# A two-layer hybrid mixer step: issue order of the first products tied by edges, a first scale chunk of two tiles, the recurrence's transposes one part later, and CV ahead of the last gate columns

## The chip, the core and the metric

The kernel runs on one core of a Trainium2 chip. The metric is the device time of one execution in microseconds; the time before is the median of three runs, 2351.44 us (2345.97 to 2354.68). The profile shows one execution on its own.

A core has five engines that each take their instructions in order from a queue of their own: TensorE (PE: matmuls; PEld is its weight load), VectorE (DVE), ScalarE (ACT), GpSimd (POOL) and SyncE (SP). SP and ScalarE also issue the transfers (DMA). An instruction that waits for a semaphore holds up everything behind it on its engine.

## The reference, cut to what matters

There are 640 tokens: 128 of context and 512 of latents, each kind with its own modulation. Two layers follow each other, each a single mixer:

```
shift, scale, gate = split(silu(cvec) @ w_ada + b_ada)
h = rms_norm(x, norm_g) * (1.0 + scale) + shift
aq, ak, av, ag, bq, bff, bfb, bi, bg, cu, cv, cg = split_proj(h @ w_in)
a_out = attend(q, k, v) * silu(ag)                 # 8 query heads, 2 kv heads, window and sink
b_out = hgrn_mixer(bq, bff, bfb, bi, bg, ...)      # recurrence, 4 heads, two directions
c_out = cu * (w_s @ layer_norm(cv) + b_s) * silu(cg)
y = concat([a_out, b_out, c_out]) @ w_out
x = x + gate * y
```

Widths: D_MODEL is 2048, w_in has 6656 columns, w_ada 6144 (2048 each of shift, scale and gate). All is float32.

## The kernel before, in words

**Tiles.** Tokens stand in NT = 5 tiles of 128, the model's 2048 inputs in KT = 16 tiles of 128 (index k). The normed and modulated input h lies transposed in 16 tiles. A float32 product is made of three cheaper ones: each operand is split into a rounded high part and the rest (hh and hl of h, wh and wl of a weight tile), and the products hh*wh, hh*wl and hl*wh are summed. `wsplit` (L617) makes wh on ScalarE (L621) and wl on VectorE (L622).

**Two forms of projection.** `rowmajor` (L644) multiplies a block of 512 columns: for each k one weight tile of 128 x 512, against the five token tiles (`mm_row`, L633 to L635), into five PSUM banks. `colmajor` (L661) makes 128 columns at a time, transposed, in two banks (`mm_col`, L641, 384 and 256 tokens).

**Side work.** Attention, the recurrence (`hgrn`, L1029) and the gating MLP (`sgu`, L1141) are generators in a list. `tick` runs the next part, up to its yield, of the first of them; a rowmajor block ticks 3 times for most weight tiles, a column tile 8 times, once per 12 of its 24 x 4 matmuls (two k). `flush` runs what is left without projection work between. `fill` runs steps of the filler: the modulation's other columns, computed on VectorE. One step loads a 128 x 512 tile of w_ada and multiplies it into two accumulators (L302). Each weight load of a projection earns `fill_rate` steps.

**What sets the order.** The kernel is written as a sequence of operations on named buffers. At compile time a scheduler orders each engine's instructions by data, free buffers, priority (`hi()` raises it) and its own estimate of when inputs will be there. Each engine then runs this order as it stands. Two calls of the library add edges that fix issue order on one engine and make no instruction wait for another to finish: `keep_in_program_order(x)` puts x behind the last instruction written on x's engine, and `issue_after(x)` puts all that a block writes on x's engine behind x.

**Layer 0's start** (`begin`, L1251). `setup` makes the silu of the conditioning and small constants; `setup2` (L195) and `prep_ctx` (L704) load the rotary tables, masks, sink logits, norm gains and cached keys and values, and convert some of them. Then `first_round` (L401). It loads x transposed in four quarters (L408). `first_norm` (L360) squares the 16 tiles on ScalarE (L366), sums over the inputs with a matrix of ones on TensorE (L368), takes Ln and Exp (L371, L372), and multiplies x by the result on VectorE, one instruction per quarter (L374). The scale half of the modulation is needed in columns, for a chunk of k at a time, `CHUNKS` (L399): 4, 4, 4, 2, 2 tiles. For a chunk, 16 tiles of w_ada (L421) are multiplied with the conditioning (`rows_mm`, L240), copied (L245), turned into columns by small products (L252) and finished on VectorE (`mod_cols`, L287 and L288). `scaled_h` (L376) then makes hh (L383) and hl (L384) of each k. So the round goes: for each chunk, its products with the key and value columns (AK, L633 to L635), with the next chunk's scale rows between them, and then the first columns of CU (L641). The shift is left out of this h and added to the results later. `second_round` (L505) makes the first query columns and computes the shift beside them; L523 and L525 evacuate its banks.

**The rest of a layer** (`layer`, L1291): the other queries, BI, CU and CG columns, then for each of four heads BFF, BFB, BQ and BG; each appends its recurrence to the side list. Then the attention gates AG 0 to 6, a flush, AG 7, CV, the gating MLP as side work under CG 1 and 2 (layer 0) or CU 0 and 1 (layer 1), a flush, and the rest of the C columns. `mul_evac` (L1179) multiplies a result by a gate: the product out of PSUM on VectorE (L1188), exp, `sigma`, and the gate's factor (L1191). `split_mix` (L1200) splits the 16 mixed tiles (L1208, L1209), and `out_proj` (L1213) projects them.

**The recurrence's loop** (L1079). Per head and token tile n: 8 small products build the two directions' attention parts (L1086), VectorE masks them (L1089) and adds them into `asum` (L1091); a yield; TensorE transposes `asum` (L1108) and ScalarE copies it (L1110); a yield; two tiles later the copy is used for the output (L1097, L1100).

Of the kernel before, what the change touches and what calls it, by code (L numbers as in the profile page):

```python
# [8 lines left out]
F32 = mybir.dt.float32  # L9
# [4 lines left out]
ALU = mybir.AluOpType  # L14
# [61 lines left out]
class Net:  # L76
# [160 lines left out]
    def rows_mm(self, acc, lhs, kk, rhs, n):  # L237

        q = kk % 4
        self.nc.tensor.matmul(acc[32 * q:32 * q + 32, 0:n], lhsT=lhs[:, kk, :], rhs=rhs, start=kk < 4, stop=kk >= 12,  # L240
                              skip_group_check=True)
# [118 lines left out]
    def first_norm(self, xm):  # L360
# [11 lines left out]
        nc.scalar.activation(r, r, AF.Exp, scale=-0.5)  # L372
        for m in xm:
            nc.vector.tensor_tensor(m, m, bc(r, 1, 4), op=ALU.mult)  # L374
# [24 lines left out]
    CHUNKS = ((0, 4), (4, 4), (8, 4), (12, 2), (14, 2))  # L399

    def first_round(self, W):  # L401
# [9 lines left out]
        def load_scale(ci):  # L411
# [3 lines left out]
            if ci >= 2:  # L415
                m = self.mg()
                raw += [m[:, i * n:(i + 1) * n] for i in range(2560 // n)]
            while len(raw) < KT:
                raw.append(self.hp.tile([P, n], F32, tag=("hh", "hl")[len(raw) % 2], name=self.nm("wa")))
            for kk in range(KT):  # L420
                nc.sync.dma_start(raw[kk], self.I["w_ada"][0, kk * P:(kk + 1) * P, D + k0 * P:D + k0 * P + n])  # L421
            return raw

        def load_w(ci):
            k0, nk = chunks[ci]
            raw = []
            for k in range(k0, k0 + nk):
                if ci in (0, 2):
# [5 lines left out]
            if ci < 4:  # L434
                if ci in (1, 3):
                    cu = self.wraw([W[k0 * P:(k0 + 4) * P, CU:CU + P]], 4, P)
                else:
                    cu = self.g(512).rearrange("p (a n) -> p a n", n=P)
                    nc.sync.dma_start(cu, W[k0 * P:(k0 + 4) * P, CU:CU + P].rearrange("(a p) n -> p a n", p=P))
                return raw, cu  # L440
            return raw, w[3][1]
# [14 lines left out]
        for ci, (k0, nk) in enumerate(chunks):  # L456
# [5 lines left out]
            raw, cu = w[ci]  # L462
            nn = chunks[ci + 1][1] if ci < last else 0
            ks = range(k0, k0 + nk)
            if ci == last:
# [4 lines left out]
                cw = self.wsplit(cu[:, 2:4], nk, P)  # L470
# [5 lines left out]
                break  # L476
            for k in ks:
                x = self.wsplit(raw[k - k0], 1, 512)
# [4 lines left out]
                for kk in range(m * (k - k0), m * (k - k0 + 1)):  # L483
                    self.rows_mm(acc, self.sc, kk, sc[ci + 1][kk], nn * P)
# [917 lines left out]
```

## Time and profile before

| what | us |
|---|---|
| median of three runs | 2351.44 |
| the profiled execution | 2357.4 |
| its span, first to last instruction | 2355.6 |
| TensorE busy | 2258.8 (96%) |
| TensorE weight load busy | 1969.0 (84%) |
| VectorE busy | 1414.7 (60%) |
| ScalarE busy | 782.5 (33%) |
| GpSimd busy | 290.0 (12%) |
| mean granted TensorE clock | 0.987 |

How to read what follows. A row of the order of time gives start, duration, engine, line, operation, output and inputs, shapes, how often, and in brackets the idle time before it with the instruction that ended it. A float32 matmul has two records. A row of waits gives who waited for whom: the sum, how often, the longest. A row of windows gives the busy time (and count) of PE, PEld, DVE, ACT and POOL in a stretch, then the granted clock, the share of the DMA engines and GB/s. SPq and ACTq are the queues of SP and ScalarE in their role as issuers of transfers.

### The profile page before, as it was taken

The numbers are of one execution on the slowest core, as the hardware profiler recorded it, in microseconds if no ns is written. First come the engines' busy times: TensorE is split into PE (matmuls) and PEld (weight loads), VectorE is DVE, ScalarE is ACT, GpSimd is POOL, SyncE is SP. The second block draws the span as 40 slices with busy tenths as digits, with TensorE's granted clock in tenths as the row PEclk, the third lists the DMA queues.
The fourth block names the chain that finished last, engine by engine and source line by source line (L and its number), as shares of the span: only waits on it lengthen the run. The fifth ranks groups of instructions, "written<-read, shape, count | busy, mean of one in ns | idle before, by whom it ended". The sixth has DMA issues, their size and how long they took to land. (4 is left out here: it accounts for less than half of the span.)

```text
span 2355.6 us, 34870 instructions
## 1 busy us (share of the span) xinstructions
PE 2258.8 (96%) x13276; PEld 1969.0 (84%) x13276; DVE 1414.7 (60%) x2605; ACT 782.5 (33%) x1603; POOL 290.0 (12%) x234
## 2 busy tenths in 40 slices
PE   4999999999999989989999999999999999999999
PEld 2676678899999989877887878799999898998887
DVE  1435887878898877874227445865775942425223
ACT  2223334344343422232224224344343432224111
POOL 0000010100322220111112010100222120101110
PEclk9999999999999999999999999999999999999999
DMA  8556733444444355555332221322332423324332
GB/s 322 182 181 205 253 115 102 141 134 123 135 134 123 113 157 160 169 186 161 108 108 81 80 64 49 104 74 71 109 95 77 121 84 94 99 77 148 103 107 85
DMA packets 262572, 296.41 MB, mean 126 GB/s; under 512 B 17122, under 2 KB 162420, under 8 KB 260612
## 3 DMA queue, kind: packets, MB, share of 16 engines
q1 hardware_dynamic: 252064, 271.27, 37.1%
q10 hardware_dynamic: 10340, 22.91, 3.1%
q8 instruction: 104, 1.70, 0.3%
q14 instruction: 64, 0.52, 0.1%
HBM read 280.38 MB, written 13.73 MB: 125 GB/s over the span
## 5 line engine op out<-in xcount | busy, mean ns | idle before, releaser
L622 DVE TENSOR_TENSOR wl<-wr,wh 128x512 fp32r<-128x512 f32 (+1 forms) x535 | 404.1, 757 | 628.6 <-ACT wh L621 619.7
L621 ACT ACTIVATE wh<-wr 128x512 fp32r<-128x512 f32 (+1 forms) x535 | 336.1, 629 | 953.8 <-PE m L635 542.2
L633 PE MATMUL m<-wh,hh 128*128 128x512 f32 x1440 | 571.6, 397 | 6.9 <-DVE mg L1188 4.2
L634 PE MATMUL m<-wl,hh 128*128 128x512 f32 x1440 | 567.8, 394 | 3.1 <-DVE wl L622 3.1
L635 PE MATMUL m<-wh,hl 128*128 128x512 f32 x1440 | 567.3, 394 | 0.0
L641 PE MATMUL m<-hh,wh 128*128 128x384 f32 x2016 | 478.2, 317 | 1.8 <-ACT g L1350 1.8
L641 PE MATMUL m<-hl,wh 128*128 128x384 f32 x2016 | 463.1, 310 | 0.0
L641 PE MATMUL m<-hh,wl 128*128 128x384 f32 x2016 | 462.6, 310 | 0.0
L302 DVE SCALAR_TENSOR_TENSOR aacc<-wa,s,aacc 128x512 f32<-128x512 f32 x480 | 364.3, 791 | 61.2 <-DMA wa<-in_w_ada_dram 60.0
L633 PEld LDWEIGHTS m<-wh,hh 128*128 128x128 f32 x1440 | 272.6, 189 | 80.4 <-issue 10.3
L635 PEld LDWEIGHTS m<-wh,hl 128*128 128x128 f32 x1440 | 273.2, 190 | 61.3 <-issue 4.9
L634 PEld LDWEIGHTS m<-wl,hh 128*128 128x128 f32 x1440 | 273.5, 190 | 59.5 <-DVE wl L622 4.1
L641 PEld LDWEIGHTS m<-hh,wh 128*128 128x128 f32 x2016 | 312.0, 190 | 9.8 <-issue 6.0
L641 PEld LDWEIGHTS m<-hh,wl 128*128 128x128 f32 x2016 | 309.7, 189 | 1.0 <-issue 0.8
L641 PEld LDWEIGHTS m<-hl,wh 128*128 128x128 f32 x2016 | 310.3, 189 | 0.3
L1071 POOL TENSOR_TENSOR mg<-ev,Dt 128x512 f32<-128x512 f32 x80 | 99.9, 1265 | 461.0 <-DMA wr<-in_w_in_dram 125.1
L1240 POOL TENSOR_TENSOR mg<-mg,ev 128x512 f32<-128x512 f32 x30 | 41.2, 1372 | 288.2 <-DVE ev L1238 284.2
L732 POOL TENSOR_TENSOR mg<-g,g 128x256 f32<-128x256 f32 x32 | 30.7, 978 | 277.3 <-DVE g L730 147.7
L906 ACT ACTIVATE g<-g,st,qs 128x384 f32<-128x384 f32 (+1 forms) x64 | 48.1, 752 | 40.6 <-DVE st L902 40.6
L922 PE MATMUL s<-misc,g 128*128 128x128 f32 x240 | 41.7, 284 | 10.9 <-DVE g L911 10.6
L228 ACT ACTIVATE ev<-ev 128x640 f32<-128x640 f32 x40 | 29.5, 738 | 65.6 <-DVE ev L227 64.4
L926 DVE TENSOR_TENSOR g<-s,g 128x512 fp32r<-128x512 f32 x56 | 38.4, 688 | 20.6 <-ACT g L925 15.0
(272 smaller groups left out, 1954.9 us busy)
## 6 DMA issues: line engine op xcount, KB each, us to landing
wr<-in_w_in_dram SPq DMA_DIRECT2D x406, 256.0 KB, 2.9
wa<-in_w_ada_dram SPq DMA_DIRECT2D x299, 256.0 KB, 2.9
wr<-in_w_out_dram SPq DMA_DIRECT2D x128, 256.0 KB, 2.6
wa<-in_w_ada_dram SPq DMA_DIRECT2D x16, 1024.0 KB, 5.7
wa<-in_w_in_dram SPq DMA_DIRECT2D x9, 1024.0 KB
mg<-const_xT_dram SPq DMA_DIRECT2D x4, 1280.0 KB, 12.8
x<-mg SPq DMA_DIRECT2D x20, 256.0 KB, 2.0
mg<-x ACTq DMA_DIRECT2D x5, 1024.0 KB
```

The costliest lines, as they stand in the source:

```text
L302: nc.vector.scalar_tensor_tensor(acc[:, cd], r, sc, acc[:, cd], op0=ALU.mult, op1=ALU.add)
L621: nc.scalar.activation(wh, raw, AF.Copy)
L622: nc.vector.tensor_tensor(wl, raw, wh.bitcast(F32), op=ALU.subtract)
L633: nc.tensor.matmul(ps, lhsT=hh, rhs=wh[:, 0], start=k == 0, stop=False)
L634: nc.tensor.matmul(ps, lhsT=hh, rhs=wl[:, 0], start=False, stop=False)
L635: nc.tensor.matmul(ps, lhsT=hl, rhs=wh[:, 0], start=False, stop=k == KT - 1)
L641: self.nc.tensor.matmul(ps[hf][:, 0:n], lhsT=w[:, a], rhs=h[:, o:o + n], start=k == 0 and i == 0, stop=k == KT - 1 and i == 2)
L906: nc.scalar.activation(dst[h], src[h], AF.Exp, bias=nmx[:, h:h + 1], scale=rq[:, h:h + 1], accum_out=den[:, h:h + 1])
L922: nc.tensor.transpose(pb[:, h * P:(h + 1) * P], dst[h][:, kb * P:(kb + 1) * P], self.ident)
L926: nc.vector.tensor_tensor(pt[1], pb, pt[0].bitcast(F32), op=ALU.subtract)
L1071: nc.gpsimd.tensor_tensor(k.rearrange("p (i c s) -> p i c s", i=4, c=4), bc(c4(pre[d][0])[:, j], 1, 4), bc(dd, 3, 32), op=ALU.mult)
L1240: (nc.vector if c == 3 else nc.gpsimd).tensor_tensor(xs, xs, y, op=ALU.add)
```

## The change

In `first_round`: the first chunk of four tiles becomes two of two, so there are six. `first_norm` returns its result r and its Exp instead of multiplying x; x is multiplied two tiles at a time (`scale_x`), a chunk ahead of its use, pinned in VectorE's program order for all but the first chunk. The weight splits of all chunks but the last, and the first copy of scale rows, are queued on ScalarE behind the norm's Exp. The scale rows of the next chunk are pinned in TensorE's program order, behind the products of the tile before them. Narrow scale tiles share a buffer.

In `begin`: `setup2` and `prep_ctx` are queued behind the last evacuations of the second round, on ScalarE and on VectorE. The filler's rate goes from 1.25 to 1.0.

In `hgrn`: tile n's `asum` is transposed in the part behind tile n + 1's attention, and its output is made at n + 3 rather than n + 2; a head has one part more.

In `layer`, for layer 0: AG 0 to 5, flush, CV, then AG 6 and 7 as cover for the gating MLP; CG 1 to 3 behind it. Layer 1 keeps its order.

```diff
-        nc.scalar.activation(r, r, AF.Exp, scale=-0.5)
-        for m in xm:
-            nc.vector.tensor_tensor(m, m, bc(r, 1, 4), op=ALU.mult)
+        last = nc.scalar.activation(r, r, AF.Exp, scale=-0.5)
+        return r, last.ins
...
-    CHUNKS = ((0, 4), (4, 4), (8, 4), (12, 2), (14, 2))
+    CHUNKS = ((0, 2), (2, 2), (4, 4), (8, 4), (12, 2), (14, 2))
...
+            i = 0
             while len(raw) < KT:
-                raw.append(self.hp.tile([P, n], F32, tag=("hh", "hl")[len(raw) % 2], name=self.nm("wa")))
+                r = self.hp.tile([P, 512], F32, tag=("hh", "hl")[i % 2], name=self.nm("wa"))
+                raw += [r[:, a:a + n] for a in range(0, 512, n)]
+                i += 1
...
+        def scale_x(ci):
+            k0, nk = chunks[ci]
+            for k in range(k0, k0 + nk, 2):
+                m = xm[k // 4][:, k % 4:k % 4 + 2]
+                x = nc.vector.tensor_tensor(m, m, bc(rrow, 1, 2), op=ALU.mult)
+                if ci > 0:
+                    self.tc.keep_in_program_order(x)
...
-        self.first_norm(xm)
+        rrow, sq = self.first_norm(xm)
         sc[1] = load_scale(1)
+        n0 = chunks[0][1]
         acc = self.bank()
         for kk in range(KT):
-            self.rows_mm(acc, self.sc, kk, sc[0][kk], 512)
-        rows = self.rows_copy(acc, 512)
-        self.mod_cols(0, 1, 0, 4, self.rows_cols(acc, rows, 512))
+            self.rows_mm(acc, self.sc, kk, sc[0][kk], n0 * P)
+        scale_x(0)
+        with self.tc.issue_after(sq):
+            rows = self.rows_copy(acc, n0 * P)
+        self.mod_cols(0, 1, 0, n0, self.rows_cols(acc, rows, n0 * P))
...
             for k in ks:
-                x = self.wsplit(raw[k - k0], 1, 512)
+                with self.tc.issue_after(sq):
+                    x = self.wsplit(raw[k - k0], 1, 512)
...
-                    self.rows_mm(acc, self.sc, kk, sc[ci + 1][kk], nn * P)
+                    self.tc.keep_in_program_order(self.rows_mm(acc, self.sc, kk, sc[ci + 1][kk], nn * P))
+            scale_x(ci + 1)
             rows = self.rows_copy(acc, nn * P)
...
-        for n in range(NT + 2):
+        aTs, sums = {}, {}
+        for n in range(NT + 3):
...
-            if n >= 2:
-                j = n - 2
+            if n >= 3:
+                j = n - 3
...
-            if n < NT:
+            if 1 <= n <= NT:
                 tb = self.bank()
-                nc.tensor.transpose(tb[:, 0:P], asum, self.ident)
+                nc.tensor.transpose(tb[:, 0:P], sums.pop(n - 1), self.ident)
...
-            self.second_round(W)
-        self.setup2()
-        self.prep_ctx(0)
+            act, dve = self.second_round(W)
+        with self.tc.issue_after(act), self.tc.issue_after(dve):
+            self.setup2()
+            self.prep_ctx(0)
...
-        self.fill_rate = 1.25
+        self.fill_rate = 1.0
...
-        for h in range(7):
+        early = 6 if l == 0 else 7
+        for h in range(early):
             self.mul_evac(self.colmajor(W, AG + h * P), self.av_view(h), True)
         self.flush()
-        for h in range(7, 8):
-            self.mul_evac(self.colmajor(W, AG + h * P), self.av_view(h), True)
+        if l > 0:
+            self.mul_evac(self.colmajor(W, AG + 7 * P), self.av_view(7), True)
         self.sgu_evac(self.rowmajor(W, CV))
         self.side.append(self.sgu(l))
         if l == 0:
-            ps = {h: self.colmajor(W, CG + h * P) for h in (1, 2)}
+            ps = [self.colmajor(W, AG + h * P) for h in (6, 7)]
             self.flush()
+            for h in (6, 7):
+                self.mul_evac(ps[h - 6], self.av_view(h), True)
```

More of the change, by code (lines that the diff above doesn't have):

```diff
@@ L239, in rows_mm @@
         q = kk % 4
-        self.nc.tensor.matmul(acc[32 * q:32 * q + 32, 0:n], lhsT=lhs[:, kk, :], rhs=rhs, start=kk < 4, stop=kk >= 12,
-                              skip_group_check=True)
+        return self.nc.tensor.matmul(acc[32 * q:32 * q + 32, 0:n], lhsT=lhs[:, kk, :], rhs=rhs, start=kk < 4, stop=kk >= 12,
+                                     skip_group_check=True)
     def rows_copy(self, acc, n):
@@ L422, in load_scale @@
             return raw
+        cu = {}
         def load_w(ci):
@@ L433, in load_w @@
                     raw.append(r.unsqueeze(1))
-            if ci < 4:
-                if ci in (1, 3):
-                    cu = self.wraw([W[k0 * P:(k0 + 4) * P, CU:CU + P]], 4, P)
-                else:
[L438 to L441, printed above, removed]
+            if k0 % 4 == 0:
+                src = W[k0 * P:(k0 + 4) * P, CU:CU + P]
+                if k0 // 4 % 2:
+                    cu[k0 // 4] = self.wraw([src], 4, P)
+                else:
+                    cu[k0 // 4] = self.g(512).rearrange("p (a n) -> p a n", n=P)
+                    nc.sync.dma_start(cu[k0 // 4], src.rearrange("(a p) n -> p a n", p=P))
+            return raw
+        def scale_x(ci):
[5 more added lines that the diff above has]
+                    self.tc.keep_in_program_order(x)
         sc, w = {}, {}
@@ L461, in first_round @@
                 sc[ci + 2] = load_scale(ci + 2)
-            raw, cu = w[ci]
-            nn = chunks[ci + 1][1] if ci < last else 0
+            raw = w.pop(ci)
+            ca = cu[k0 // 4][:, k0 % 4:k0 % 4 + nk]
             ks = range(k0, k0 + nk)
@@ L469, in first_round @@
                     self.scaled_h(k, xm[k // 4][:, k % 4])
-                cw = self.wsplit(cu[:, 2:4], nk, P)
+                cw = self.wsplit(ca, nk, P)
                 for k in ks:
@@ L522, in second_round @@
             if t % 2:
-                nc.vector.tensor_copy(a, ps[t])
+                dve = nc.vector.tensor_copy(a, ps[t])
             else:
-                nc.scalar.activation(a, ps[t], AF.Copy)
+                act = nc.scalar.activation(a, ps[t], AF.Copy)
+        return act.ins, dve.ins
     def bias_rows(self, W):
@@ L1091, in hgrn @@
                 nc.vector.tensor_tensor(asum, self.att[0], self.att[1], op=ALU.add)
+                sums[n] = asum
                 if n + 1 < NT:
                     K = build(n + 1)
-            if n >= 2:
-                j = n - 2
+            if n >= 3:
+                j = n - 3
                 oo = self.bank()
```

12 lines of the change are left out of this document (5 added, 7 removed).

## The prediction

> **What bounds the kernel now.** I read the page first, then TensorE's waits, then the order of time at the start, then windows around each long wait.
>
> ```profile
> span 2355.6 us, 34870 instructions
> ...
> PE 2258.8 (96%) x13276; PEld 1969.0 (84%) x13276; DVE 1414.7 (60%) x2605; ACT 782.5 (33%) x1603; POOL 290.0 (12%) x234
> ...
> L302 DVE SCALAR_TENSOR_TENSOR aacc<-wa,s,aacc 128x512 f32<-128x512 f32 x480 | 364.3, 791 | 61.2 <-DMA wa<-in_w_ada_dram 60.0
> ...
> mg<-const_xT_dram SPq DMA_DIRECT2D x4, 1280.0 KB, 12.8
> ```
>
> TensorE is busy in 2258.8 of 2355.6 us. The change removes no matmul work, so it can win only the 96.8 us in which TensorE idles, and what its clock loses after an idle stretch. The waits say where that time lies:
>
> ```profile
> PE s L1108 <- DVE asum L1091: 22.4, 12, 5.7
> PE s L368 <- ACT g L366: 17.4, 1, 17.4
> PE s L166 <- DVE g L159: 16.7, 1, 16.7
> PE s L922 <- DVE g L911: 10.6, 8, 3.5
> PE m L633 <- DVE mg L1188: 4.2, 1, 4.2
> ```
>
> Three of the five are in places that the diff touches: the recurrence's transposes (L1108), the norm's sums (L368), and layer 0's first output products, which wait for the last gate's evacuation (L1188). What stands at the start, on TensorE:
>
> ```profile
> 34.77 20.01 PE L368 MATMUL s<-g,ones 128*128 128x384 f32 x64 [17.39 <-ACT g L366]
> 54.71 4.48 PE L240 MATMUL s<-wa,pad 128*32 128x512 f32 x34
> 59.15 1.05 PE L252 MATMUL s<-misc,g 128*128 128x2 f32 x8
> 60.13 3.63 PE L240 MATMUL s<-wa,pad 128*32 128x512 f32 x30
> 64.53 1.05 PE L252 MATMUL s<-misc,g 128*128 128x2 f32 x8 [0.76 <-ACT g L245]
> 67.93 0.79 PE L633 MATMUL m<-wh,hh 128*128 128x512 f32 x1 [2.35 <-ACT hh L383]
> ```
>
> and on ScalarE and VectorE:
>
> ```profile
> 33.47 0.63 ACT L621 ACTIVATE wh<-wr 128x512 fp32r<-128x512 f32 x1 [15.04 <-DMA wr<-in_w_in_dram]
> 34.00 4.48 ACT L366 ACTIVATE g<-mg 128x640 f32<-128x640 f32 x7
> ```
>
> ```profile
> 56.13 11.03 DVE L374 TENSOR_TENSOR mg<-mg,g 128x2560 f32<-128x2560 f32 x4 [15.81 <-ACT g L372]
> 67.08 0.23 DVE L287 SCALAR_TENSOR_TENSOR gs<-s,cols 128x8 f32<-128x8 f32 x2
> ```
>
> Here is the reading that matters most. The norm's squares (L366) do not wait for x. ScalarE takes its instructions in order, and the first weight split (L621) stands ahead of the squares and waits 15.04 us for a weight tile that is loaded last. Once it is free, the squares run seven in a row, so x had been there. Then VectorE multiplies all of x in one block of 11.03 us, and the small scale columns (L287), on which the first product hangs, queue behind it.
>
> **The start.** When could the squares begin?
>
> ```profile
> 1.18 0.42 SPq L408 DMA_DIRECT2D mg<-const_xT_dram x1
> ...
> 7.35 1.30 SPq L408 DMA_DIRECT2D mg<-const_xT_dram x3
> 8.70 18.72 SPq L421 DMA_DIRECT2D wa<-in_w_ada_dram x16
> ```
>
> x's first quarter is issued at 1.18 and the page gives 12.8 us to its landing: 14.0 us. The others, issued by 8.65, land by 21.5 at the same 12.8, and the norm, at 20.01/16 = 1.25 us a tile, asks for the last quarter only 12 tiles or 15 us after its start. With the split queued behind the norm's Exp, the first square ends at 14.0 + 4.48/7 = 14.7, and the sums, at the same 20.0 us, end at 34.7 in place of 54.7. That is the step I trust most; its bounds are 8 us (x as fast as its issue allows, since the moved setup loads no longer share the queue, sums ending near 29) and 21.5 (all of x needed first, sums ending near 42).
>
> From there to the first product. TensorE does 16 scale rows of 256 columns rather than 512:
>
> ```profile
> 105.39 1.06 PE L240 MATMUL s<-wa,pad 128*32 128x512 f32 x8
> ...
> 114.41 0.64 PE L240 MATMUL s<-mg,pad 128*32 128x256 f32 x8
> ```
>
> By 0.64/1.06 these take 0.60 of the 3.63 us, 2.2 us. Then the copy with its hand-over, 64.53 - 63.76 = 0.77; four small column products, half of 1.05, 0.5; and from the scale columns to the first product 67.93 - 67.08 = 0.85. Sum 4.3 us. VectorE's side is shorter: from the sums' end to the multiply's start 56.13 - 54.72 = 1.4, and two of sixteen tiles cost 11.03/8 = 1.4. The two weight splits that now come after the Exp fit between on ScalarE (0.63 us each). So the first product comes at 39.0, not at 67.93: 28.9 us earlier.
>
> Not all of this is won. Before its first product the old kernel had also done the second chunk's rows and columns, 3.63 + 1.05, and half of the first chunk's, 2.2 + 0.5: 7.4 us of matmuls that hid under the 11 us multiply and now stand between products. Two more chunk boundaries appear, each with the copy, columns and scale to pass under two column tiles; the bounds are 0 and the 2.35 of the old first wait, and I take 0.5 each, since the old boundaries inside the round show no wait. Net 28.9 - 7.4 - 1.0 = 20.5 us.
>
> The multiplies that leave the block are 1.4 us each in VectorE's slack between products. SP's queue gains 16 more, smaller issues; 16 whole ones took 18.72 us while waiting for the setup's small loads, and half the bytes have until 34.7. Here a rule of the Trainium skill speaks against the change: DMA: Bandwidth & Descriptors, section Bandwidth, says to batch transfers to 1 MiB or more, and its fit gives 2.3 us for 128 KB; one after another, 16 such would land near 46 us and put the first product at 50, 11 us of the gain lost. The row above disagrees with the "one after another": 16 transfers of 256 KB were issued in 18.72 us, so they overlapped, at 1.2 us each.
>
> The clock is a second point:
>
> ```profile
> 60.00:80.00 20.00, 16.89 (x81) 11.71 (x82) 13.53 (x19) 7.07 (x15) 0.00 (x0) 0.83 0.74 243
> 820.00:840.00 20.00, 14.35 (x115) 13.06 (x114) 17.73 (x28) 4.79 (x10) 6.97 (x6) 0.91 0.50 148
> 1020.00:1040.00 20.00, 12.74 (x43) 9.31 (x43) 15.97 (x24) 5.79 (x10) 1.68 (x1) 0.83 0.70 248
> 1880.00:1900.00 20.00, 15.46 (x124) 13.92 (x125) 11.41 (x26) 4.83 (x12) 9.69 (x9) 0.83 0.23 63
> ```
>
> After idling 0.76 + 2.35 us the granted clock means 0.83 over 20 us, a loss of 3.4 us. The new gap is 4.3 - 2.2 - 0.5 = 1.6 us, shorter; but nothing here says that it is short enough, and I let the 3.4 us stand. The Trainium skill (TensorE: Matmul & The Clock Gate, What's actually happening) has the clock fall only after an idle window of about 3.4 us; by that the start would win 3.4 us more.
>
> **The recurrence.** The sum of the two attention parts is transposed one part later.
>
> ```profile
> 835.82 0.45 PE L1108 MATMUL s<-misc,asum 128*128 128x128 f32 x1 [5.65 <-DVE asum L1091]
> ```
>
> ```profile
> 1884.54 0.45 PE L1108 MATMUL s<-misc,asum 128*128 128x128 f32 x1 [5.47 <-DVE asum L1091]
> ```
>
> ```profile
> 1894.37 1.76 PE m L641 x12
> ```
>
> Between two parts of a head lie 12 projection matmuls, 1.76 us. The transpose now follows its sum by three such stretches rather than one, so it has 3.5 us more (two by 1.76). Of the 12 waits the two longest keep 5.65 - 3.5 and 5.47 - 3.5, together 4.1; the ten others sum to 22.4 - 11.1 = 11.3, mean 1.1, and go. That is 18.3 us, and with the clock (0.91 and 0.83 over 20 us lose 1.8 and 3.4) up to 23.5. But VectorE is late at these places (17.73 of 20 us busy, and the filler's multiplies wait 60.0 us in all for their loads, in VectorE's queue). Some of the lateness will come up at the next thing that TensorE wants from it; I take two thirds of 23.5, 15 us. Bounds: 0 and 23.5. A head needs one part more, 35 rather than 34, four heads 140; the columns ahead of the flush offer 144 in layer 0 (18 tiles by 8), so nothing spills out.
>
> **The end of layer 0.** CV moves ahead of AG 6 and 7, and these cover the gating MLP in place of CG 1 and 2; so all three CG tiles lie between it and the output projection, rather than one.
>
> ```profile
> 1022.12 3.75 DVE L1209 TENSOR_TENSOR hl<-mg,hh 128x640 fp32r<-128x640 f32 x5
> 1025.80 0.87 DVE L1188 TENSOR_TENSOR mg<-mg,m 128x384 f32<-128x384 f32 x2
> ```
>
> VectorE reached the last evacuation (L1188) only after five splits, while TensorE needed its bank. The window from 1020 has 7.3 us idle and 3.4 us of clock lost, 10.7. With two more tiles of cover the earlier gates are out of the way, but the splits still end in the same order. I take half, 5 us; bounds 0 and 10.7.
>
> **The filler's rate, 1.25 to 1.0 steps a weight load.** A step is two multiplies of 0.791 us, so VectorE has a fifth less of it while layer 0 projects, and more in the output projection. A fifth of the 10.6 us of attention waits is 2 us; bounds 0 and 5.
>
> **The setup behind the second round.** Nine loads on ScalarE's queue, and VectorE's conversions that wait for them, now come after the evacuation of the first query half. Queued behind them are ScalarE's weight splits, and TensorE waits for these.
>
> ```profile
> ACT mg L525 <- DMA g<-in_cache_k_dram: 2.1, 1, 2.1
> ```
>
> Four of the nine stood there already, and one held ScalarE for 2.1 us, with no wait on TensorE. I charge 2 us; bounds 0 and 10 (five more by 2.1).
>
> **Sum.** -20.5 - 15 - 5 - 2 + 2 = -40.5 us. The profiled execution took 2357.4 us, so 2316.9 for such a one; it stood 0.25% above the median of the runs, and the same ratio, 0.983, on 2351.44 gives 2311.
>
> **Rivals.** *The recurrence gains nothing* (0.13): VectorE's lateness is work, not order, and TensorE waits as long at the next evacuation. For it: VectorE's 17.73 of 20 us. Against: at 1880 it is busy 11.41 of 20 only. -40.5 + 15: 2326.
>
> *The start gains nothing* (0.08): the scale rows arrive late, because their smaller loads wait for one another, and the first product stays where it was. For it: 18.72 us went into issuing 16 loads. Against: a weight tile issued behind x and a whole scale chunk had landed by 33.47, before the sums' new end at 34.7. -40.5 + 20.5: 2331. The rule on batching above would make half of this loss.
>
> *All waits in reach go* (0.06): 28.9 - 7.4, 23.5, 10.7, 5: about -61, 2291.
>
> *The edges do not give the order that they name, or the rest of the program is ordered anew and new waits eat the gain* (0.09): 2347.
>
> *Slower* (0.05): pinned scale rows stall the products.
>
> ```profile
> SPq L421 <- PE s L240: 15.3, 5, 7.6
> ```
>
> Each chunk's rows are now tied behind the products before them, and the next products stand behind the rows on TensorE. If a chunk's loads come late, because the loads wait for buffers (five times, up to 7.6 us), TensorE waits too. At all five boundaries, with the clock's 3.4 us: 5 x 11 = 55 us, -40.5 + 55 = +14.5: 2366. It decides from 40.5/5 - 3.4 = 4.7 us a boundary (7.1 for half a percent). Against it: these waits of SP left TensorE without a wait.
>
> **Chances.** Forecast 0.59, rivals as given. Half a percent, 11.8 us, is about what a measurement of this kernel can tell from no change. Faster: 0.59 + 0.13 + 0.08 + 0.06 = 0.86; same 0.09; slower 0.05. The forecast's own range, from the bounds of the unknown costs, is 2296 to 2326. The range given reaches the two smaller gains and the largest, 2288 to 2338.
>
> **What would show it.** Right: the squares start near 14 us, the sums end near 35, the first product (the old L633) starts near 39; the sum of waits for asum is under 6 us; the wait for the last gate's evacuation is shorter. Wrong: the squares still begin behind a weight split; a wait of the scale rows for loads; waits for attention or weight splits that grew by what asum's lost.

## The result, and the profile after

The changed kernel takes 2338.84 us (median of 7 runs, 2336.47 to 2342.52), the kernel before 2353.25 in the same comparison; the ratio is 0.9945, 95% interval 0.9931 to 0.9960. That is 13 us or 0.55% faster, just beyond what a measurement can tell from no change, where 40 us were forecast; the time lies 0.8 us outside the range. One run of the kernel before at 2788 us, and one at 5726 us in the comparison of runs 13 to 16, are left out of the ratios; without the first, its median is 2352.3 us. The profiled execution took 2338.18 us.

First the page of the kernel after: its span, the busy times, the filler's multiplies and the loads of x.

```profile
span 2336.4 us, 34944 instructions
...
PE 2261.4 (97%) x13308; PEld 1968.0 (84%) x13308; DVE 1424.3 (61%) x2612; ACT 778.7 (33%) x1605; POOL 293.9 (13%) x234
...
L302 DVE SCALAR_TENSOR_TENSOR aacc<-wa,s,aacc 128x512 f32<-128x512 f32 x480 | 368.6, 801 | 72.9 <-DMA wa<-in_w_ada_dram 72.3
...
mg<-const_xT_dram SPq DMA_DIRECT2D x4, 1280.0 KB, 5.8
```

TensorE is as busy as before (2261.4 against 2258.8 us), so the 19.2 us between the two spans are idle time. The filler's multiplies wait longer for their loads, 72.3 us instead of 60.0. That goes with the lower rate: of the runs below with two buffers and all loads, those at 1.25 have 60.5 (run 1) and 53.7 (run 4), those at 1.0 between 70.7 and 78.5. Why is open. The start, on TensorE and then on ScalarE:

```profile
11.96 19.26 PE L368 MATMUL s<-g,ones 128*128 128x384 f32 x64 [1.72 <-DVE g L184]
31.15 1.93 PE L240 MATMUL s<-wa,pad 128*32 128x256 f32 x32
33.90 0.61 PE L252 MATMUL s<-misc,g 128*128 128x2 f32 x4 [0.81 <-ACT g L245]
35.94 0.73 PE L652 MATMUL m<-wh,hh 128*128 128x512 f32 x1 [1.44 <-ACT hh L382]
```

```profile
11.06 0.21 ACT L181 ACTIVATE g<-g 128x16 f32<-128x16 f32 x1 [1.89 <-DVE g L180]
11.19 4.47 ACT L366 ACTIVATE g<-mg 128x640 f32<-128x640 f32 x7
```

The squares start at 11.19 us (34.00 before), right behind the setup's last activation (L181), which waits for VectorE; the sums end at 31.2 (54.7), the first product (L633 before, L652 now) starts at 35.94 (67.93): 32.0 us earlier. Because some matmuls that used to hide now stand between products, the fair measure is a count: the 400th projection matmul (L633 to L635 and L641 before, L652 to L654 and L660 after) ends 24.5 us earlier than before. The same count taken further down both traces tells where the lead goes: 26.5 us at the 2000th, 37.9 at the 3400th, in the last head of layer 0's recurrence, 28.3 at the 3552nd, the last before the two kernels go on with different columns, 21.0 at the 4272nd, where layer 0's columns end, 16.1 at the 5200th, near the end of layer 0's output projection, and 19.2 at the end. So the recurrence did win another 11 us, and lost 9.6 of them at its last step. Part of such a lead can be side work that is only put off. TensorE's idle time up to the same products leaves that out: it is shorter than before by 23.2, 24.4, 33.0, 26.7, 22.2, 21.3 and 21.8 us at these seven places. What it was lost to, TensorE's waits say (engine, line waited for, us in total, times, longest):

```profile
PE s L1143 <- DVE g L1137: 10.4, 6, 6.1
PE s L166 <- DVE g L159: 9.5, 1, 9.5
PE s L941 <- DVE g L930: 8.7, 6, 3.2
PE s L1072 <- ACT g L1068: 7.7, 2, 4.1
PE m L652 <- DVE mg L1208: 5.3, 1, 5.3
PE s L1193 <- DVE mg L1194: 5.1, 1, 5.1
...
PE s L1128 <- DVE att L1108: 1.9, 1, 1.9
```

The wait for `asum`, 22.4 us before, is gone altogether. In its place stand three that before had 0.3, 0 and 0: a head's last transposes wait for the scaling of their input (L1143 for L1137), the products on kT for its copy (L1072 for L1068), and the moved transposes for the attention copy (L1128 for L1108). These are 10.4 + 7.7 + 1.9 = 20.0 us. The wait at the last gate's evacuation is 5.3 rather than 4.2, and the gating MLP's output (L1193) waits 5.1 rather than 1.0. What VectorE did ahead of the longest of them:

```profile
835.18 2.74 DVE L302 SCALAR_TENSOR_TENSOR aacc<-wa,s,aacc 128x512 f32<-128x512 f32 x4 [2.05 <-DMA wa<-in_w_ada_dram]
837.84 0.28 DVE L1124 COPY g<-s 128x128 f32<-128x128 f32 x1
...
840.86 4.01 DVE L302 SCALAR_TENSOR_TENSOR aacc<-wa,s,aacc 128x512 f32<-128x512 f32 x4 [0.94 <-DMA wa<-in_w_ada_dram]
844.79 0.68 DVE L641 TENSOR_TENSOR wl<-wr,wh 128x512 fp32r<-128x512 f32 x1
845.40 0.28 DVE L1124 COPY g<-s 128x128 f32<-128x128 f32 x1
845.60 0.73 DVE L302 SCALAR_TENSOR_TENSOR aacc<-wa,s,aacc 128x512 f32<-128x512 f32 x1
846.26 1.06 DVE L1137 TENSOR_SCALAR g<-g,oss 128x128 f32<-128x128 f32 x5
```

```profile
846.59 0.47 PE L1143 MATMUL s<-misc,g 128*128 128x128 f32 x1 [6.08 <-DVE g L1137]
```

VectorE takes its queue in order. Ahead of the last output copy (L1124) and the scaling (L1137) stand eight filler multiplies in two groups, 6.75 us of work, with 2.05 and 0.94 us of waiting for their loads. The Trainium skill says the same of the queue (Perfetto Trace Analysis, the section Per-engine timelines: VectorE, ScalarE and GpSimd are strictly first in, first out), and this trace agrees: TensorE had finished the last product to be copied at 834.75 us (L1120), and its copy starts at 845.40. The other wait, for the kT copy, runs over ScalarE:

```profile
1839.73 0.75 ACT L1206 ACTIVATE ev<-m 128x384 f32<-128x384 f32 x2
1845.53 0.74 ACT L228 ACTIVATE ev<-ev 128x640 f32<-128x640 f32 x1 [5.05 <-DVE ev L227]
1846.30 0.74 ACT L229 ACTIVATE ev<-ev 128x640 f32<-128x640 f32 x1
1846.94 0.61 ACT L640 ACTIVATE wh<-wr 128x512 fp32r<-128x512 f32 x1
1847.46 0.58 ACT L1068 ACTIVATE g<-s 128x512 f32<-128x512 f32 x1
```

A column tile ends at 1839.7. Its evacuation needs VectorE (L227), which is late; ScalarE stands 5.05 us behind that, and the kT copy stands behind ScalarE's evacuation, though TensorE's transposes for it (L1067) had run from 1841.93 for 0.60 us. The stretches with these waits also lose clock (the windows' rows; the third number from the end is the mean granted clock, the last two are the DMA share and GB/s):

```profile
840.00:860.00 20.00, 13.92 (x74) 13.07 (x73) 16.33 (x29) 4.97 (x12) 1.96 (x1) 0.83 0.48 144
930.00:950.00 20.00, 14.82 (x89) 14.63 (x90) 16.86 (x30) 2.78 (x6) 0.03 (x1) 0.83 0.51 157
1000.00:1020.00 20.00, 13.67 (x52) 10.47 (x51) 15.67 (x23) 9.30 (x17) 3.76 (x3) 0.83 0.65 221
```

0.83 over 20 us is at most 3.4 us lost in each. Some of it falls into the idle time itself: in the first window the clock is at half from 845.0 to 851.6 us, and TensorE idles until 846.6.

### The profile page after: what moved, and what is told of

Same layout as the page of the kernel before. It is cut to its first block, busy times and chain, and to the rows that moved or that the text cites. A ratio compares the mean times of both kernels' runs of the same rounds, so it can differ in the third digit from the quotient of the medians.

```text
span 2336.4 us, 34944 instructions
## 1 busy us (share of the span) xinstructions
PE 2261.4 (97%) x13308; PEld 1968.0 (84%) x13308; DVE 1424.3 (61%) x2612; ACT 778.7 (33%) x1605; POOL 293.9 (13%) x234
## 4 chain that ended last, share of the span: by engine, by line
PE 75%; DVE 12%; DMA 7%; issue 2%; ACT 1%; POOL 0%; DVEq 0%; ACTq 0%; POOLq 0%
PE m L660 29%; PE m L652 11%; PE m L653 11%; PE m L654 11%; DMA wa<-in_w_ada_dram 6%; DVE aacc L302 4%; DVE wl L641 2%; PE s L240 2%; PE s L895 1%; PE s L941 1%; PE s L1105 1%; PE s L1072 1%; PE s L953 1%; PE s L954 1%; PE s L319 1%
## 5 line engine op out<-in xcount | busy, mean ns | idle before, releaser
L641 DVE TENSOR_TENSOR wl<-wr,wh 128x512 fp32r<-128x512 f32 (+1 forms) x535 | 401.5, 752 | 575.2 <-ACT wh L640 566.7
L652 PE MATMUL m<-wh,hh 128*128 128x512 f32 x1440 | 571.6, 397 | 9.2 <-DVE mg L1208 5.3
L654 PE MATMUL m<-wh,hl 128*128 128x512 f32 x1440 | 565.6, 393 | 0.0
L660 PE MATMUL m<-hh,wh 128*128 128x384 f32 x2016 | 478.1, 317 | 0.0
L660 PE MATMUL m<-hl,wh 128*128 128x384 f32 x2016 | 465.0, 311 | 0.0
L660 PE MATMUL m<-hh,wl 128*128 128x384 f32 x2016 | 464.6, 311 | 0.0
L302 DVE SCALAR_TENSOR_TENSOR aacc<-wa,s,aacc 128x512 f32<-128x512 f32 x480 | 368.6, 801 | 72.9 <-DMA wa<-in_w_ada_dram 72.3
L652 PEld LDWEIGHTS m<-wh,hh 128*128 128x128 f32 x1440 | 272.0, 189 | 84.5 <-issue 10.3
L654 PEld LDWEIGHTS m<-wh,hl 128*128 128x128 f32 x1440 | 272.4, 189 | 59.0 <-issue 2.6
L660 PEld LDWEIGHTS m<-hh,wh 128*128 128x128 f32 x2016 | 312.5, 190 | 9.8 <-issue 8.1
L660 PEld LDWEIGHTS m<-hl,wh 128*128 128x128 f32 x2016 | 311.5, 189 | 0.4
L660 PEld LDWEIGHTS m<-hh,wl 128*128 128x128 f32 x2016 | 311.1, 189 | 0.3
L1090 POOL TENSOR_TENSOR mg<-ev,Dt 128x512 f32<-128x512 f32 x80 | 95.7, 1213 | 321.5 <-PE s L1105 107.2
L228 ACT ACTIVATE ev<-ev 128x640 f32<-128x640 f32 x40 | 29.5, 738 | 72.3 <-DVE ev L227 71.2
L945 DVE TENSOR_TENSOR g<-s,g 128x512 fp32r<-128x512 f32 x56 | 38.4, 687 | 24.0 <-ACT g L944 18.1
L1045 POOL TENSOR_TENSOR g<-g,EG 128x512 f32<-128x512 f32 x16 | 22.7, 1416 | 239.4 <-DVE Dt L1030 125.1
```

What stands on the lines that cost most here:

```text
L302: nc.vector.scalar_tensor_tensor(acc[:, cd], r, sc, acc[:, cd], op0=ALU.mult, op1=ALU.add)
L641: nc.vector.tensor_tensor(wl, raw, wh.bitcast(F32), op=ALU.subtract)
L652: nc.tensor.matmul(ps, lhsT=hh, rhs=wh[:, 0], start=k == 0, stop=False)
L654: nc.tensor.matmul(ps, lhsT=hl, rhs=wh[:, 0], start=False, stop=k == KT - 1)
L660: self.nc.tensor.matmul(ps[hf][:, 0:n], lhsT=w[:, a], rhs=h[:, o:o + n], start=k == 0 and i == 0, stop=k == KT - 1 and i == 2)
L945: nc.vector.tensor_tensor(pt[1], pb, pt[0].bitcast(F32), op=ALU.subtract)
```

## The experiments

Each run is set against the kernel before on the same chip; ratios have their 95% interval. Line numbers differ by one or two between the kernels. "Parts" are the pieces into which a head's work is cut, laid between column matmuls.

**1. The new start alone**: the changed kernel with the loop, the column order and the rate of before; the setup edge stays.

```diff
-        for n in range(NT + 3):
+        for n in range(NT + 2):
...
-        self.fill_rate = 1.0
+        self.fill_rate = 1.25
...
-        early = 6 if l == 0 else 7
-        for h in range(early):
+        for h in range(7):
```

> The kernel before with the first round's edges and two-tile chunks and with the setup behind the second round; recurrence, columns' order and filler rate as before. Theory A (VectorE's lateness only moves): the start is worth what the profiles show at the 400th projection matmul, 24 us, and the rest of the change nothing or less, so this is 24 us below the kernel before, about 2329, faster than the changed kernel. Theory B (the recurrence is worth the 15 us that were forecast, and another part of the change takes them back): the same 2329 here, since neither is in it. Theory C (a rebuilt order is worth plus or minus 10 us whatever is edited): anywhere from 2320 to 2345.

Measured: 2332.7 us, 0.9912 (0.9894 to 0.9930). The start by itself is faster than the whole change. The other edits together cost about 6 us.

**2, 3, 4. One edit undone each**, in the changed kernel: the old loop (2), the old column order (3), the old rate (4).

```diff
-                nc.tensor.transpose(tb[:, 0:P], sums.pop(n - 1), self.ident)
+                nc.tensor.transpose(tb[:, 0:P], asum, self.ident)
```

> The changed kernel with the old recurrence loop. Theory A: the waits go back from the last transposes (L1143 of the changed kernel) to those of asum, and the time stays, 2339 plus or minus 4. Theory B: 15 us slower than the changed kernel, 2354.

Measured: 2331.8 us, 0.9906 (0.9888 to 0.9924). The new loop costs 7 us. The waits of the kernel with the old loop:

```profile
PE s L1127 <- DVE asum L1110: 9.9, 6, 5.3
...
PE s L1142 <- DVE g L1136: 4.1, 2, 3.9
```

With 1.4 us of waiting for GpSimd (L1105 for L1090) these are 15.4 us in the recurrence, where the new loop has 20.0. Neither expectation had a gain.

```diff
-            ps = [self.colmajor(W, AG + h * P) for h in (6, 7)]
+            ps = {h: self.colmajor(W, CG + h * P) for h in (1, 2)}
```

> The changed kernel with AG 7 before CV and CG 1 and 2 under the gating MLP, as before. Theory A: the wait for the last evacuation ahead of the output projection is about as long either way (4.2 before, 5.3 after), so 2339 plus or minus 4. Theory B, the forecast's own term: 5 us slower, 2344.

Measured: 2331.2 us, 0.9908 (0.9888 to 0.9927). The new order costs 7.7 us, which neither expectation had; without it the wait at the gating MLP is gone from the list, and the one at the last evacuation is 4.6 us.

> The changed kernel with the filler at 1.25 steps again. The profiles lose about 8 us between the 1400th and the 2000th row product, in layer 0's output projection, where the filler now runs on. Theory A: with 1.25 it ends sooner there and some of the 8 us come back, but VectorE is later in the recurrences: 2330 to 2340. Theory B with the filler as the part that takes the gain back: 2329. The forecast's own term for the rate: 2 us slower, 2341.

Measured: 2338.6 us, 0.9936 (0.9921 to 0.9952): no difference. With the new loop and order, the rate is worth nothing.

**5, 6. Filler without its loads**: fifteen of sixteen loads of the filler's weight tiles are left out, in the changed kernel (5) and with the old loop (6). Every multiply is still done, on a tile that is there already, so the gates and layer 1's modulation are not the reference's.

```diff
-            with self.hi():
-                r = self.arp.tile([P, 512], F32, tag="ar", name=self.nm("wa"))
+            if k == 0:
+                with self.hi():
+                    r = self.arp.tile([P, 512], F32, tag="ar", name=self.nm("wa"))
```

> The changed kernel, but each of the filler's blocks loads one tile and multiplies it sixteen times: 15 of 16 of the filler's loads are left out, so its outputs (gates, and layer 1's modulation) are not the reference's; all multiplies stay. Theory A, in the form that the filler's load waits in VectorE's queue (72 us in all after the change) put VectorE late: TensorE's waits for L1137, L1194, L1208 and L1068 (28 us after the change) fall below 10, and the time to 2315 or less. Theory A2, that the filler's multiplies alone (369 us) are what stands ahead: the waits stay above 18, 2332 or more.

> The same as the kernel with one load a block (15 of 16 filler loads left out), with the old recurrence loop. If VectorE is no longer late (theory A), the position of the transposes is worth under 4 us either way against that kernel. Theory B, the forecast's: the old loop waits for asum again, 10 to 15 us slower than that kernel.

Measured: 2304.9 us (5; 0.9789, 0.9771 to 0.9807) and 2292.6 (6; 0.9736, 0.9716 to 0.9757). The loads are worth 34 us of the whole. Not all of this need be their waits: 63 of 296 MB of traffic are gone with them (the pages of the two kernels). The new loop costs 12 us without them too, which neither expectation had, so they are not what makes it slow. Its rows in 5, and then those of 6:

```profile
PE s L1144 <- DVE g L1138: 6.0, 5, 2.2
PE s L1129 <- DVE att L1109: 5.4, 3, 3.3
PE s L1073 <- ACT g L1069: 5.0, 2, 2.5
```

```profile
PE s L1128 <- DVE asum L1111: 7.3, 8, 1.7
...
PE s L1106 <- POOL mg L1091: 2.2, 4, 0.8
```

16.4 against 9.5 us, and none of the old loop's waits for `asum` is longer than 1.7. The gating MLP's wait fell to 1.3 in 5 and that of the last evacuation to 3.1: those two do come from the loads. The four waits that run 5 was to bring from 28 us to below 10 (for the scaling, the kT copy, the gating MLP and the last evacuation) still make 15.4.

**7. Start, setup edge and rate**, with the old loop and the old order (the first run with the rate at 1.0).

```diff
-        self.fill_rate = 1.25
+        self.fill_rate = 1.0
```

> The kernel before with the start's edges, the setup behind the second round and the filler at 1.0; recurrence and columns' order as before. If the parts are separate: undoing the recurrence alone won 7 us and undoing the columns' order alone 7.7, so both undone is 2339 - 14.7 = 2324. If the two shared one cause (each undone removes the same loss): 2332, as the start alone gave. Theory C, order by luck: outside 2320 to 2336.

Measured: 2321.6 us, 0.9859 (0.9841 to 0.9877). Here the rate is worth 11 us, five times what the forecast gave it. The `asum` rows of run 1, and then of run 7, show where:

```profile
PE s L1127 <- DVE asum L1110: 22.1, 12, 5.7
```

```profile
PE s L1127 <- DVE asum L1110: 9.7, 6, 5.3
...
PE s L1142 <- DVE g L1136: 4.2, 2, 3.9
```

Rate and loop were aimed at the same wait, and the rate takes 12.4 of its 22.1 us; 4.2 come up at the scaling.

**8, 9, 11. A third buffer for the filler's loads**, on run 7; room for it comes from single buffers for `So` and `asum` and a scratch tile done away with.

```diff
-        self.arp = ec(tc.tile_pool(name="arp", bufs=2))
+        self.arp = ec(tc.tile_pool(name="arp", bufs=3))
```

> The kernel with the start's edges and the filler at 1.0, recurrence and order as before, and three buffers rather than two for the filler's loads; to make room, asum and the state copy have one buffer and the squares of the recurrence's output are written into its output tile. Theory A (load waits make VectorE late): the filler's load waits fall from over 60 to under 25 us and the time by 5 to 10 us below the same kernel with two buffers. If the loads are late for another reason (their place in SP's queue, behind other waits): no change, plus or minus 4.

Measured: 2328.2 us, 0.9886 (0.9865 to 0.9907), slower. The filler began inside the start:

```profile
50.09 0.79 PE L652 MATMUL m<-wh,hh 128*128 128x512 f32 x1 [15.01 <-ACT hh L382]
```

So in 9 the filler's first multiply is tied behind the second round, and 11 adds the new column order.

```diff
-                    nc.vector.tensor_scalar(acc[:, cd], r, sc, None, op0=ALU.mult)
+                    with self.tc.issue_after(self.behind) if (l, blk) == (0, 8) else nullcontext():
+                        nc.vector.tensor_scalar(acc[:, cd], r, sc, None, op0=ALU.mult)
```

> The kernel with three filler buffers, with one more edge: the filler's first multiply is queued on VectorE behind the second round. Without that edge the third buffer put filler work into the start (TensorE waited 20 us for L382 there), but from the 400th projection matmul on that kernel was 16 us faster than the one with two buffers. Theory A (load waits make VectorE late): the start is whole again and the 16 us stay, 2306 plus or minus 4. If the 16 us came from the filler having begun early: 2318 to 2322.

> The kernel with three filler buffers and the tied filler, with the new columns' order (CV ahead of AG 6 and 7). If the order's cost of 8 to 10 us came from the filler's load waits beside the gating MLP: within 3 us of the same kernel with the old order. If it lies in the order itself: 8 to 10 us slower than that.

Measured: 2312.7 us (9; 0.9823, 0.9806 to 0.9841) and 2312.1 (11; 0.9820, 0.9803 to 0.9838). The load waits in VectorE's queue, in the waits of run 9:

```profile
DVE aacc L303 <- DMA wa<-in_w_ada_dram: 18.1, 14, 4.8
```

18.1 us rather than 75.2 in run 7, and the new order now costs nothing and brings nothing, where with the same loop and two buffers it costs 10 us (run 2 against run 7): its loss in the change came from late loads. These are the fastest of the kernels that compute the whole reference, 26 us below the changed one.

**10. One part more at the tail**: run 3 (new loop, old order) with an empty part ahead of a head's last transposes, 36 parts a head.

```diff
             nc.vector.tensor_scalar(oj, oj, ss[:, j:j + 1], None, op0=ALU.mult)
         yield
         yield
+        yield
```

> The changed kernel with the old columns' order (2331.2) and the new recurrence loop, with one empty part more ahead of a head's last transposes, so that VectorE's scaling (L1137) has 1.76 us more. If the new loop's cost of 7 to 12 us lies at that place alone: 5 us or more faster, 2326 or less. Theory A (lateness only moves to whatever asks next): the waits for L1137 shrink, others grow, 2331 plus or minus 4.

Measured: 2314.8 us, 0.9841 (0.9819 to 0.9863), 16 us faster than run 3. The recurrence's waits of run 3, then of run 10:

```profile
PE s L1143 <- DVE g L1137: 11.7, 6, 7.7
...
PE s L1072 <- ACT g L1068: 7.1, 2, 3.9
...
PE s L1128 <- DVE att L1108: 1.9, 1, 1.9
```

```profile
PE s L1128 <- DVE att L1108: 3.8, 2, 1.9
PE s L1144 <- DVE g L1137: 3.6, 3, 2.8
```

20.7 us became 7.4. The scaling's wait was to go and mostly went; that the kT copy's went too was not expected.

**12. The setup edge taken off** run 7.

```diff
-        with self.tc.issue_after(act), self.tc.issue_after(dve):
-            self.setup2()
-            self.prep_ctx(0)
+        self.setup2()
+        self.prep_ctx(0)
```

> The kernel with the start's edges and the filler at 1.0 (2321.6), with the setup and the cached keys free to be issued early again. Their place behind the second round costs 2.7 us of wait for the cached keys and 1.7 us of clock; at the start, their small loads held SP's queue for 10 us before. If the edge only costs: 2317. If it is what lets x come early: the first sums end some us later and the time is 2322 to 2328.

Measured: 2321.7 us, 0.9864 (0.9847 to 0.9882). The edge is worth nothing; the traces show two effects that about cancel. Without it VectorE waits until 10.20 us for the load of the attention sinks (L220), ahead of the silu of the conditioning, and the first product comes at 37.82 us rather than 35.45 in run 7. With it, TensorE waits 2.7 us for the cached keys (L738) in run 7, and in run 12 it does not.

**13 and 14. The part more elsewhere**: in run 7, with the old loop (13, 35 parts), and in the changed kernel whole (14, 36 parts); the edit is that of run 10.

> The kernel with the new start, the setup edge and rate 1.0, the old recurrence loop and the old column order (2321.6 us without this edit), with one empty part more before a head's last transposes. If the extra part alone made the gain of 16 us of the kernel with the new loop and that part, this one comes out near 2314 (2311 to 2317), and the later asum transposes are worth nothing. If the later transposes pay only once the tail has a part more, this one stays at 2321.6 (within 4), because the old loop waits 9.7 us for the asum tile and only 4.2 for the scaling, and the part takes away those 4.2 at most.

> The changed kernel whole (new column order too) with one empty part more before a head's last transposes. If the tail was what the new loop lost by, in any order: 2338.8 less the 16 us that the same edit gave with the old order, 2323 (2318 to 2328). If the new order's load waits take the gain back (the wait of 5.1 us at the gating MLP and 5.3 at the last evacuation stay): nearer 2330.

Measured: 2322.9 us (13; 0.9855, 0.9831 to 0.9879) and 2325.3 (14; 0.9862, 0.9842 to 0.9882). With the old loop the part brings nothing; in the changed kernel it brings 13.5 us by the medians. And in 13 a wait appears that the old loop with 34 parts does not have:

```profile
PE s L1072 <- ACT g L1068: 7.1, 2, 4.7
```

Every run with 35 parts a head, the old loop or the new, has this wait (4.9 to 7.7 us), none with 34 or 36 does. A column tile holds eight parts; the number of parts sets where the fourth head's kT products fall against a tile's end.

**15 and 16. Third buffer and part more**: run 9 with the part at the tail (16), and with the new loop as well (15; two `asum` buffers, made room for by narrower constant tiles).

> Third filler buffer tied behind the second round (2312.7 us with the old loop), with the new loop and the extra part at the tail, old column order. The new loop's two edits together gave 7 us against the old loop where loads were late; with loads in time the asum waits that they take away are 6.7 us in 8. If that holds with three buffers: 2306 (2302 to 2310). If TensorE in layer 0 is bound by VectorE's total work up to the gating MLP, so that waits only move: 2312 (within 3).

> Third filler buffer tied behind the second round, old loop, with the extra part at the tail alone. The profile without that part shows one wait of 5.2 us for the scaling and 6.7 us for the asum tile. If the part takes away the first: 2307 (2304 to 2310); if the wait moves to the asum tile or to the last evacuation: 2312 (within 3).

Measured: 2321.3 us (15; 0.9842, 0.9824 to 0.9861) and 2319.3 (16; 0.9844, 0.9822 to 0.9866), against 0.9823 for run 9: both miss, and the two gains do not add up. Run 16 has 35 parts and the kT wait (5.9 us). In run 15 the moved transposes wait 7.4 us for the attention copy.

**17 and 18. The same number of parts, placed otherwise**: the empty part at a head's start rather than its tail, in run 3 (17), and two of them in run 7, with the old loop (18). Both have 36.

```diff
         pre = []
+        yield
```

> The kernel with the new loop and the old column order (2331.2 us), with the empty part more at the start of each head rather than at its tail: 36 parts a head, the tail as it was. If the gain of 16 us came from the room ahead of the last transposes, it is not here: 2331 (2327 to 2334). If it came from where the parts fall against the column tiles of eight parts (with 35 parts the fourth head's products on kT fall one part behind a tile's end, with 34 and 36 they don't), it is here too: 2315 (2312 to 2319), and TensorE's wait for the kT copy, 7.1 us in 2, is gone.

> The kernel with the new start, the setup edge, rate 1.0, the old loop and the old column order (2321.6 us with 34 parts a head, 2322.9 with 35), with two empty parts at the start of each head: 36. If the later transposes are worth nothing once the number of parts is alike, this one equals the kernel with the new loop and 36 parts, 2315 (2312 to 2318). If the number of parts matters only with the later transposes, it stays at 2322 (2319 to 2325). No wait for the kT copy in either case.

Measured: 2327.6 us (17; 0.9883, 0.9864 to 0.9903) and 2330.5 (18; 0.9895, 0.9879 to 0.9912). The rows of 17, then those of 18:

```profile
PE s L1129 <- DVE att L1109: 8.4, 3, 3.1
...
PE s L1144 <- DVE g L1138: 4.5, 1, 4.5
PE m L660 <- DVE ev L988: 3.9, 2, 2.7
```

```profile
PE s L1129 <- DVE asum L1112: 19.4, 18, 2.3
...
PE s L1144 <- DVE g L1138: 3.0, 1, 3.0
```

In 17 the kT wait is gone as the theory of parts had it, but only 3.6 us of the time, within the uncertainty: most of run 10's gain hung on the place at the tail. In 18 the old loop is 9 us slower with 36 parts than with 34; neither expectation had that. The wait for `asum` doubled, 9.7 to 19.4 us, though the part that follows the sum is the same: only the place against the column tiles moved. The six kernels that differ only in loop and parts, from their traces; the waits are all the idle time ahead of the recurrence's own products and transposes (us):

| loop, parts a head | waits in the recurrence | TensorE idle in all | time |
|---|---|---|---|
| new, 36, at the tail (10) | 7.7 | 52.5 | 2314.8 |
| old, 34 (7) | 15.2 | 59.8 | 2321.6 |
| old, 35, at the tail (13) | 17.3 | 61.4 | 2322.9 |
| new, 36, at the start (17) | 14.5 | 65.6 | 2327.6 |
| old, 36, at the start (18) | 22.4 | 70.8 | 2330.5 |
| new, 35 (3) | 21.1 | 65.6 | 2331.2 |

The time follows TensorE's idle time, roughly, and neither the loop nor the number of parts alone. The waits in the recurrence are not all of it: in 17, column tiles wait 3.9 us for an evacuation (L660 for L988) besides. With 36 parts in both and the empty ones at the start, the new loop has 8 us less waiting than the old (17 against 18), and 2.9 us less time, which the two intervals do not tell from none.

## Why the prediction was right in direction and wrong in size

**The start** was forecast at -20.5 us. Run 1 gives -22 (2332.7 against 2354 to 2355), the trace's count 24.5. Its mechanism held: the squares stand no longer behind the split, and the sums end at 31.2 (34.7 forecast) and the first product starts at 35.9 (39.0). One reading in it was wrong. x does not set the squares' start: its first quarter lands 6.1 us after its issue rather than 12.8, at 7.3 us, and the squares begin at 11.19 behind the setup's work, 2.8 us before the forecast's 14.0; that is the 3. The pauses ahead of the first product are 2.25 us where 1.6 were forecast. The sixteen smaller loads overlapped, as the row of before had said: sixteen were issued in 14.60 us, each took 3.3 us to land (median of the page), and no scale row waited for them. The rival *slower*, pinned rows that stall, did not come.

**The step that failed is the recurrence's**: "Some of the lateness will come up at the next thing that TensorE wants from it; I take two thirds of 23.5, 15 us. Bounds: 0 and 23.5." The first half was right and better than forecast: `asum`'s wait fell from 22.4 to nothing (with the rate at 1.25 too, run 4). But 20.0 us came up elsewhere, at the scaling and the kT copy above all, and the lower bound of 0 left out a loss. Beside the old loop in the same kernel, the edit cost 7 us (run 2), 10 with the old order (run 3 against 7) and 12 without loads (5 against 6).

What the runs show in place of the step is that the waiting moves to whatever TensorE wants next, and that its sum depends on where a head's parts fall. The step counted the part more as free, since 140 parts fit in 144 slots. It moved the heads' steps against the tiles' ends: at 35 parts the kT copy queues behind an evacuation that waits for VectorE (7.7 us here; 7.1 with the old loop in 13, where other waits shrank and the time stayed). One part more at the tail brings 16 and 13.5 us back with the new loop (10 and 14) and nothing with the old (13); two empty parts cost the old loop 9 us (18); and against that one the new loop, also with 36 parts and its empty one at the start, loses nothing (17). So the 7 to 12 us are the price of the later transposes together with their part, and not of later transposes as such.

That the old wait had been cover, in which VectorE and ScalarE caught up ahead of the head's tail, fits the gain of the part at the tail, but no run shows it by itself. The rival *the recurrence gains nothing* had the mechanism, lateness as work. Its argument against, VectorE only 11.41 of 20 us busy, failed because the 20 us reach far behind the wait: in the kernel before, during the wait of 5.47 us that ends at 1884.54, VectorE was busy from 1879.43 to 1884.39, and in the rest of the window it stood 6.4 us waiting for TensorE's products (L1086).

**The end of layer 0** was forecast at -5 with bounds 0 and -10.7; it cost 7.7 (run 3), or 10 with the old loop (run 2 against 7). The wait at the last evacuation went from 4.2 to 5.3 and a second one, 5.1, came at the gating MLP. Run 11 shows that the order is neutral once the loads are in time.

**The rate** was sized at -2 from attention's waits (L922 before), which it left nearly alone (10.5 in run 1, 9.1 in run 7). It acts on `asum`: -11 with the old loop and order (run 7), 0 with the new ones (run 4). The sum added two edits that act on the same wait.

**The setup edge** was charged 2 and is worth 0 (run 12): the charge was about right (2.7), but the 2 us that the edge wins at the start were left out.

By the runs, step by step: -22 (run 1), -11 (run 7), +10 (the new loop, run 3), +8 (the new order, the changed kernel): -15 or so, and 13 to 14 are measured. Such steps run from one kernel to the next and must add up; in another order the shares differ. With the rate at 1.25, for one, the new loop and order together cost 6 us (run 4 against run 1) rather than 17.

Open is why one placing of the parts has less waiting than another, beyond the kT copy; the rows name the waits, but no run predicts them. Every edit also lets the scheduler order the program anew, and empty parts alone moved the time by up to 9 us, so a difference of that size between two of these kernels need not come from what its edit was meant to do. That the moved transposes wait for the attention copy because it frees one of the few small banks was argued from the order and not tried. Why runs 15 and 16 lose against run 9 beyond their kT and attention waits is open too.

## What to carry to other kernels

A wait taken away on the bound engine is a gain only if the next thing that it wants is ready by then: before pricing it, write down what the late engine still owes behind it, with what stands ahead in its queue, and let the lower bound go below nothing. Two edits that shorten the same wait are priced together, not added. Filler that waits for its own loads in an in-order queue delays everything behind it; one more buffer, kept out of the start, was worth more here than two reorderings.

## What the runs showed of the hardware

The clock falls after short pauses. In the kernel after, pauses of 0.81 and 1.44 us (the start, above) stand ahead of the window in the first row; in the kernel before, the two pauses of the second view stand just ahead of the window of the third and in it:

```profile
36.00:46.00 10.00, 10.00 (x50) 7.14 (x54) 4.05 (x6) 2.06 (x5) 0.00 (x0) 0.83 1.01 353
```

```profile
438.11 0.39 PE L641 MATMUL m<-hh,wh 128*128 128x256 f32 x1 [1.76 <-ACT g L1350]
...
442.19 0.69 PE L922 MATMUL s<-misc,g 128*128 128x128 f32 x2 [1.42 <-DVE g L911]
```

```profile
438.00:448.00 10.00, 8.44 (x35) 6.78 (x36) 7.67 (x17) 4.15 (x13) 0.00 (x0) 0.66 0.70 216
```

0.83 over 10 us is 1.7 us lost, and 0.66 is at most 3.4 (the second pause falls into the slow stretch), without any pause of 2 us. In the kernel before, the clock fell ahead of the second pause: read by single microseconds it is 1.00 up to 439, 0.62 from 439 to 440 and 0.50 from there to 446, and TensorE had worked without a pause from 430 to the first one. The Trainium skill (TensorE: Matmul & The Clock Gate, What's actually happening) gives an idle window of about 3.4 us as what it takes; here a pause of 1.76 us did, as far as the trace's modelled ends of matmuls tell.

One small load at the head of VectorE's queue moved the whole start. In run 12 the conversion of the attention sinks (L220) waited for its load until 10.20 us, and the silu's step behind it (L227) ran at 10.28, where it runs at 8.28 in the changed kernel; the squares followed at 13.19 rather than 11.19. The first quarter of x had taken 5.9 us there and 6.1 in the changed kernel, so x was not what was late.
